# The walk of the 512-column products: runs of 16 columns from four places, or runs of 4 from thirty-two

## The chip, the cores and the metric

One core of one Trainium2 chip runs the whole program; the other cores do nothing. The metric is the device time of one execution in microseconds (us), the median of several runs. The engines of the core that matter here are TensorE (the matrix engine; its profile rows are PE for the product itself and PEld for loading the stationary operand), VectorE (DVE), ScalarE (ACT) and GpSimd (POOL). TensorE keeps one operand of 128x128 standing still, streams the columns of the other past it, and adds the result up in PSUM, whose banks hold 512 single-precision columns per partition.

## The reference

Three blocks of a transformer-like network run one after the other on one sequence of 512 positions of width 1024. Each part of a block is changed by a shift, a scale and a gate, which come from a product of a conditioning vector with a large matrix.

- A first block: a gated feed-forward part, `swiglu(y) = (silu(y @ w_gate) * (y @ w_up)) @ w_down` with a hidden width of 2816, then a mixer of four mLSTM heads and four HGRN2 heads, then a second such feed-forward part.
- A second block: gated linear attention with four heads, then `square(relu(h @ w1)) @ w2` with a hidden width of 4096.
- A third block: differential attention with eight heads and rotary positions, then the same kind of feed-forward part, then a last normalisation.

Everything is single precision. Nearly all of the arithmetic lies in products of a 512-row activation with a weight matrix; the recurrences and attention scores use many small products.

## The kernel before, in words

A large product is made in three. Each operand is split into two parts of the type float32r, a high part and a low part (the rest), and the kernel adds high by high, high by low and low by high into one PSUM bank. For weights `parts2` does the split: ScalarE copies the high part into a tile named `w` (line 118 is the helper that all ScalarE work goes through) and VectorE subtracts (line 328). Activations are kept as pairs of tiles, in the regions that the profile calls XAr and XBr.

Two functions issue these products:

- `fm` (lines 372 to 374) has a 128-column block of the weight standing and lets the 512 positions stream. Its result lies with features on partitions.
- `tm` (lines 390 to 392) has 128 positions of the activation standing and lets 512 columns of the weight stream. Its result lies with positions on partitions.

Both loop over the 128-row pieces of the contraction, three products each. Every product has its own load of a stationary operand, which runs beside the product before it. The order on TensorE is the program's order; there is no planner at run time. Background work (the conditioning products on VectorE) is put between the products by counting them, so that the order of instructions does not depend on how long a product takes.

Where the streaming operand has 512 columns, the function `runs` turns both it and the PSUM result into a view with the columns in another order. The view `(a b c) -> b a c` with a=4 and c=16 makes b=8: sixteen neighbouring columns (64 bytes) are taken from the first place, then sixteen from a place 128 columns (512 bytes) further, and so on over four places; then the four places each move on by sixteen columns. That makes 32 runs of 16. Operand and result use the same view, so that every column of the result is where it would be without it. Views of any other width are left as they are: at the beginning of most stages the positions come in two halves of 256 (`HALVES`), and the last 512 columns of the output come as two times 256; these walk straight through.

The small products (scores, transposes, recurrences) do not go through `runs`.

Of the kernel before, what the change touches and what calls it, by code (L numbers as in the profile page):

```python
# [35 lines left out]
def kernel(ctx: ExitStack, tc: tile.TileContext, a: dict, out: bass.AP):  # L36
# [321 lines left out]

    def runs(ap):

        return ap.rearrange("p (a b c) -> p b a c", a=4, c=16) if ap.shape[1] == 512 else ap

    def fm(p, wt, X, span, c=0):

        s, n = span
        kn = wt.shape[2]
        work(0.65 * kn * n / 512)
        for k in range(kn):
            xh, xl = X[k]
            wh, wl = wt[:, 0, k, c:c + 128], wt[:, 1, k, c:c + 128]  # L370
            xh, xl = runs(xh[:, s:s + n]), runs(xl[:, s:s + n])
            PE.matmul(runs(p), lhsT=wh, rhs=xh, start=k == 0, stop=False)  # L372
            PE.matmul(runs(p), lhsT=wh, rhs=xl, start=False, stop=False)  # L373
            done = PE.matmul(runs(p), lhsT=wl, rhs=xh, start=False, stop=k == kn - 1)  # L374
        products.append(done)
        if len(products) == due[0]:
            flush((1, 1, 1, 1))
# [1290 lines left out]
```

## Time and profile before

| what | value |
|---|---|
| median of 3 runs | 2318.18 us (2316.72 to 2320.07) |
| the profiled execution | 2320.75 us |
| its span, first to last instruction | 2319.0 us |
| instructions | 27,962 |
| mean granted clock of TensorE | 0.996 |
| TensorE products | busy 2262.5 us, 10,904 instructions |
| stationary loads | busy 1846.2 us, 10,904 instructions |
| VectorE | busy 1413.5 us |
| ScalarE | busy 924.0 us |
| read from HBM | 290.78 MB, 126 GB/s over the span |

The busy time of TensorE counts a product from its first fetch to a modelled end, and neighbours overlap: one product reads as 0.39 us while the next one starts 0.23 us after it. For a stream of products the useful number is therefore the distance from one start to the next. A timeline gives it: the first and the last start of a stretch, divided by the number of steps between.

### The profile page before, as it was taken

The numbers are of one execution on the slowest core, as the hardware profiler recorded it, in microseconds if no ns is written. First come the engines' busy times: TensorE is split into PE (matmuls) and PEld (weight loads), VectorE is DVE, ScalarE is ACT, GpSimd is POOL, SyncE is SP. The second block draws the span as 40 slices with busy tenths as digits, with TensorE's granted clock in tenths as the row PEclk, the third lists the DMA queues.
The fourth block names the chain that finished last, engine by engine and source line by source line (L and its number), as shares of the span: only waits on it lengthen the run. The fifth ranks groups of instructions, "written<-read, shape, count | busy, mean of one in ns | idle before, by whom it ended". The sixth has DMA issues, their size and how long they took to land.

```text
span 2319.0 us, 27962 instructions
## 1 busy us (share of the span) xinstructions
PE 2262.5 (98%) x10904; PEld 1846.2 (80%) x10904; DVE 1413.5 (61%) x2371; ACT 924.0 (40%) x1722; POOL 191.2 (8%) x126
## 2 busy tenths in 40 slices
PE   6999999999899999999999999999999999999998
PEld 4888887888788888888878887888776767888887
DVE  7846455765767746555555765658746577634364
ACT  4332224644665232234543532322435456333222
POOL 0111111000101111010000010101000100100000
PEclk9999999999999999999999999999999999999999
DMA  9755444435323655442332254445341322423231
GB/s 273 235 176 180 146 164 73 110 103 104 95 75 108 209 166 171 128 162 82 124 114 91 93 186 148 149 134 157 126 135 43 114 64 74 136 91 103 88 92 63
DMA packets 212900, 294.69 MB, mean 127 GB/s; under 512 B 7257, under 2 KB 120328, under 8 KB 212768
## 3 DMA queue, kind: packets, MB, share of 16 engines
q1 hardware_dynamic: 212128, 291.85, 41.2%
q8 instruction: 85, 1.39, 0.3%
q10 hardware_dynamic: 640, 1.07, 0.1%
q14 instruction: 47, 0.39, 0.1%
HBM read 290.78 MB, written 2.11 MB: 126 GB/s over the span
## 4 chain that ended last, share of the span: by engine, by line
PE 86%; DVE 6%; ACT 3%; DMA 2%; issue 1%; POOL 1%; POOLq 0%; SPq 0%; ACTq 0%; DVEq 0%
PE PS L392 13%; PE PS L390 13%; PE PS L391 13%; PE PS L372 13%; PE PS L373 13%; PE PS L374 13%; PE PS L1474 1%; DVE w L328 1%; POOL sm L413 1%; PE PS L907 1%; ACT RS L118 1%; PE PS L1503 1%; DMA araw<-in_ada_w_dram 1%; ACT tmp L118 1%; ACT XBf L118 1%
## 5 line engine op out<-in xcount | busy, mean ns | idle before, releaser
L328 DVE TENSOR_TENSOR w<-raw,w 128x1024 fp32r<-128x1024 f32 (+1 forms) x392 | 470.9, 1207 | 416.8 <-ACT w L118 415.8
L118 ACT ACTIVATE w<-raw 128x1024 fp32r<-128x1024 f32 (+1 forms) x392 | 389.2, 1000 | 512.3 <-PE PS L392 287.3
L373 PE MATMUL PS<-XAr,w 128*128 128x512 f32 (+1 forms) x1328 | 488.8, 368 | 0.9 <-DVE XAr L696 0.4
L374 PE MATMUL PS<-XAr,w 128*128 128x512 f32 (+1 forms) x1328 | 488.1, 368 | 0.0
L372 PE MATMUL PS<-XAr,w 128*128 128x512 f32 (+1 forms) x1328 | 485.5, 369 | 0.5 <-DVE XAr L471 0.5
L390 PE MATMUL PS<-w,XAr 128*128 128x512 f32 x806 | 319.9, 398 | 3.3 <-DVE XAr L471 2.5
L391 PE MATMUL PS<-w,XAr 128*128 128x512 f32 x806 | 318.0, 395 | 0.0
L392 PE MATMUL PS<-w,XAr 128*128 128x512 f32 x806 | 316.2, 393 | 0.0
L373 PEld LDWEIGHTS PS<-XAr,w 128*128 128x128 f32 x1328 | 251.5, 189 | 43.4 <-DVE XAr L696 1.2
L372 PEld LDWEIGHTS PS<-XAr,w 128*128 128x128 f32 x1328 | 250.4, 189 | 43.9 <-ACT XAr L118 1.3
L374 PEld LDWEIGHTS PS<-XAr,w 128*128 128x128 f32 x1328 | 251.4, 189 | 41.4
L392 PE MATMUL PS<-w,XBr 128*128 128x512 f32 x704 | 277.9, 395 | 3.0 <-DVE XBr L612 2.5
L391 PE MATMUL PS<-w,XBr 128*128 128x512 f32 x704 | 278.4, 395 | 0.0
L390 PE MATMUL PS<-w,XBr 128*128 128x512 f32 x704 | 277.7, 395 | 0.1
L118 ACT ACTIVATE tmp<-PS 128x512 f32<-128x512 f32 (+3 forms) x227 | 104.5, 466 | 416.6 <-PE PS L374 324.3
L245 DVE SCALAR_TENSOR_TENSOR acc<-araw,silu_c,acc 128x512 f32<-128x512 f32 x266 | 199.2, 749 | 70.7 <-DMA araw<-in_ada_w_dram 66.5
L253 POOL PARTITION_ALL_REDUCE tmp<-acc x38 | 133.6, 3516 | 1054.4 <-DVE acc L245 542.6
L390 PEld LDWEIGHTS PS<-w,XAr 128*128 128x128 f32 x806 | 151.9, 189 | 37.5 <-DVE XAr L471 2.7
L392 PEld LDWEIGHTS PS<-w,XAr 128*128 128x128 f32 x806 | 151.9, 189 | 34.4 <-issue 0.8
L391 PEld LDWEIGHTS PS<-w,XAr 128*128 128x128 f32 x806 | 152.1, 189 | 33.6 <-issue 1.6
L392 PEld LDWEIGHTS PS<-w,XBr 128*128 128x128 f32 x704 | 132.2, 188 | 34.1 <-DVE XBr L612 3.4
L390 PEld LDWEIGHTS PS<-w,XBr 128*128 128x128 f32 x704 | 132.1, 188 | 32.5 <-ACT RS L118 0.5
(293 smaller groups left out, 2491.1 us busy)
## 6 DMA issues: line engine op xcount, KB each, us to landing
araw<-in_ada_w_dram SPq DMA_DIRECT2D x152, 512.0 KB
raw<-in_mlp_w_dram SPq DMA_DIRECT2D x56, 1024.0 KB
raw<-in_ffn_w_gate_dram SPq DMA_DIRECT2D x20, 1024.0 KB
raw<-in_ffn_w_up_dram SPq DMA_DIRECT2D x20, 1024.0 KB
raw<-in_ffn_w_down_dram SPq DMA_DIRECT2D x20, 1024.0 KB
raw<-in_w_in_dram SPq DMA_DIRECT2D x16, 1024.0 KB
raw<-in_gla_w_in_dram SPq DMA_DIRECT2D x12, 1024.0 KB
raw<-in_diff_w_in_dram SPq DMA_DIRECT2D x12, 1024.0 KB
```

The costliest lines, as they stand in the source:

```text
L118: ins = S.activation(out, in_, func, **kw)
L245: V.scalar_tensor_tensor(acc, raw[:, k, :], col, acc, op0=ALU.mult, op1=ALU.add)
L253: G.partition_all_reduce(red, acc, channels=128, reduce_op=bass_isa.ReduceOp.add)
L328: V.tensor_tensor(wt[:, 1, ks], src[:, ks], wt[:, 0, ks].bitcast(F32), op=ALU.subtract)
L372: PE.matmul(runs(p), lhsT=wh, rhs=xh, start=k == 0, stop=False)
L373: PE.matmul(runs(p), lhsT=wh, rhs=xl, start=False, stop=False)
L374: done = PE.matmul(runs(p), lhsT=wl, rhs=xh, start=False, stop=k == kn - 1)
L390: PE.matmul(runs(p), lhsT=xh[:, s:s + 128], rhs=wh, start=n == 0, stop=False)
L391: PE.matmul(runs(p), lhsT=xh[:, s:s + 128], rhs=wl, start=False, stop=False)
L392: done = PE.matmul(runs(p), lhsT=xl[:, s:s + 128], rhs=wh, start=False, stop=n == last)
L413: G.tensor_tensor(r, ms, mhalf[:, 0:w], op=ALU.pow)
L907: PE.matmul(p[:, c * 128:(c + 1) * 128], lhsT=L[:, c * 128:(c + 1) * 128], rhs=R[:, c * 128:(c + 1) * 128], start=True, stop=True)
```

## The change

One line in `runs`. The view keeps its form, but the sizes given are b=4 and c=4, which makes a=32: four neighbouring columns (16 bytes) are taken from the first place, then four from a place 16 columns (64 bytes) further, over thirty-two places; then all places move on by four columns. That makes 128 runs of 4. Both operand and result are walked this way. Nothing else differs: the same products, the same operands, the same tiles and order.

```diff
     def runs(ap):
 
-        return ap.rearrange("p (a b c) -> p b a c", a=4, c=16) if ap.shape[1] == 512 else ap
+        return ap.rearrange("p (a b c) -> p b a c", b=4, c=4) if ap.shape[1] == 512 else ap
```

## Rows read from the trace of the kernel before

**Rows 1.** The page, part 1: busy us, share of the span, instructions.
```profile
PE 2262.5 (98%) x10904; PEld 1846.2 (80%) x10904; DVE 1413.5 (61%) x2371; ACT 924.0 (40%) x1722; POOL 191.2 (8%) x126
```
**Rows 2.** The page, part 4: the chain that ended last, by engine and by line.
```profile
PE 86%; DVE 6%; ACT 3%; DMA 2%; issue 1%; POOL 1%; POOLq 0%; SPq 0%; ACTq 0%; DVEq 0%
PE PS L392 13%; PE PS L390 13%; PE PS L391 13%; PE PS L372 13%; PE PS L373 13%; PE PS L374 13%; PE PS L1474 1%; DVE w L328 1%; POOL sm L413 1%; PE PS L907 1%; ACT RS L118 1%; PE PS L1503 1%; DMA araw<-in_ada_w_dram 1%; ACT tmp L118 1%; ACT XBf L118 1%
```
**Rows 3.** Groups by line and form, TensorE products: count, busy us, mean ns, idle.
```profile
L372 PE MATMUL PS<-XAr,w 128*128 128x512 f32 x1008 | 395.6, 396 | 0.0
L390 PE MATMUL PS<-w,XAr 128*128 128x512 f32 x794 | 316.5, 399 | 3.3 <-DVE XAr L471 2.5 <-DVE XAr L833 0.7
L390 PE MATMUL PS<-w,XBr 128*128 128x512 f32 x704 | 277.7, 395 | 0.1
L372 PE MATMUL PS<-XAr,w 128*128 128x256 f32 x320 | 89.9, 283 | 0.5 <-DVE XAr L471 0.5
L372 PE MATMUL PS<-XBr,w 128*128 128x512 f32 x208 | 81.7, 393 | 0.0
```
**Rows 4.** PE waits, longest in total first: us, times, longest.
```profile
PE PS L907 <- DVE tmp L935: 8.2, 3, 7.0
PE PS L209 <- DMA tmp<-in_ffn_pre_g_dram: 6.2, 1, 6.2
```
**Rows 5.** Timeline, `fm` streaming XA: first and last of 176 rows (start, us).
```profile
299.67 0.39 PE L374 MATMUL PS<-XAr,w 128*128 128x512 f32 x1
...
339.93 0.39 PE L372 MATMUL PS<-XAr,w 128*128 128x512 f32 x1
```
**Rows 6.** Timeline, `tm` with XB standing: first and last of 156 rows.
```profile
229.81 0.40 PE L390 MATMUL PS<-w,XBr 128*128 128x512 f32 x1
...
265.81 0.40 PE L392 MATMUL PS<-w,XBr 128*128 128x512 f32 x1
```
**Rows 7.** Timeline, `tm` with XA standing: first and last of 153 rows.
```profile
2074.72 0.39 PE L392 MATMUL PS<-w,XAr 128*128 128x512 f32 x1
...
2109.80 0.39 PE L391 MATMUL PS<-w,XAr 128*128 128x512 f32 x1
```
**Rows 8.** Timeline, seven products in a row near 1700 us.
```profile
1698.09 0.63 PE L391 MATMUL PS<-w,XAr 128*128 128x512 f32 x1
...
1700.65 0.63 PE L391 MATMUL PS<-w,XAr 128*128 128x512 f32 x1
```
**Rows 9.** Windows: PE, PEld, DVE, ACT, POOL busy (x), granted clock, DMA share, GB/s.
```profile
1697.80:1701.10 3.30, 3.30 (x10) 2.53 (x9) 3.01 (x7) 1.02 (x2) 0.00 (x0) 0.50 0.55 159
225.00:268.00 43.00, 43.00 (x187) 34.74 (x186) 24.72 (x30) 7.95 (x8) 7.29 (x2) 1.00 0.52 168
270.00:356.00 86.00, 86.00 (x375) 70.49 (x374) 47.29 (x62) 26.08 (x34) 16.45 (x25) 1.00 0.48 159
```
**Rows 10.** Timeline, `fm` in halves of 256, straight: first and last of 156 rows.
```profile
1334.78 0.28 PE L372 MATMUL PS<-XAr,w 128*128 128x256 f32 x1
...
1352.96 0.28 PE L374 MATMUL PS<-XAr,w 128*128 128x256 f32 x1
```
**Rows 11.** Timeline, `tm` on 256 columns, straight: first and last of 36 rows.
```profile
2307.66 0.28 PE L390 MATMUL PS<-w,XAr 128*128 128x256 f32 x1
...
2311.86 0.27 PE L392 MATMUL PS<-w,XAr 128*128 128x256 f32 x1
```
**Rows 12.** Timeline, `fm` in gated linear attention: first and last of 89 rows.
```profile
1184.54 0.39 PE L374 MATMUL PS<-XAr,w 128*128 128x512 f32 x1
...
1205.07 0.39 PE L372 MATMUL PS<-XAr,w 128*128 128x512 f32 x1
```

## The prediction

> **What bounds the kernel now.** I read the page from the top. TensorE is busy for 98% of the span, VectorE for 61%, ScalarE for 40% [rows 1], so the first question is whether TensorE waits for anybody. The chain that ended last lies on TensorE for 86%, and six lines of `fm` and `tm` hold 13% each, 78% together [rows 2]. The list of waits agrees: the largest are 8.2 and 6.2 us [rows 4]. So the time is the number of products times the distance from one start to the next, and the page's mean of 0.39 us is not that distance, since neighbours overlap.
>
> The number comes from the groups by form. `fm` has 1008 + 208 products of 512 columns on line 372, `tm` has 794 + 704 on line 390 [rows 3]; each stands on three lines, so 3648 and 4494, together 8142. The distance comes from the timeline. Streaming XA, `fm` makes 175 steps in 339.93 - 299.67 = 40.26 us, 0.2301 us each [rows 5]. `tm` makes 155 steps in 36.00 us with XB standing, 0.2323 [rows 6], and 152 in 35.08 us with XA standing, 0.2308 [rows 7]; weighted with the counts 0.2315. 8142 products at about 0.231 us are 1880 us, 81% of the span. A step of 1 ns in that distance is worth 8.1 us.
>
> Then the question that decides: does a product take longer than its columns? Where the granted clock is 0.50 (1.2 GHz), six steps take 1700.65 - 1698.09 = 2.56 us, 0.4267 each [rows 8, 9]: 512 columns at one per cycle, to the last nanosecond. At 2.4 GHz the same would be 0.2133. The stretches at a granted 1.00 [rows 9] show 0.2301 and 0.2315, so 16.8 and 18.2 ns of a product are lost at the high level that are not lost at the low one. The 32 runs of the walk are there at both levels, so the loss is a supply that falls short of one column per cycle at 2.4 GHz. On that supply the order of the columns can act.
>
> **The change part by part.** No instruction is removed, added or moved: the same products and loads, the same bytes into the same places of PSUM, so that DMA, VectorE and ScalarE have the same work. The only term is the distance of 8142 products.
>
> No row shows runs of 4, so I bound them. From below: the whole loss goes, 3648 x 16.8 ns + 4494 x 18.2 ns = 61 + 82 = 143 us. From above: the whole loss is the price of the 32 runs, 0.53 and 0.57 ns each; 96 more runs then cost 50.4 and 54.6 ns, 184 + 245 = 429 us.
>
> Between these ends the nearest rows are the products that walk straight. `fm` on 256 columns makes 155 steps in 18.18 us, 0.1173 each [rows 10]; `tm` on 256 makes 35 in 4.20 us, 0.1200 [rows 11]. If what is lost grows with the columns, 512 straight columns would take 0.2346 and 0.2400, more than the 0.2301 and 0.2315 of the walk. Runs would then help: from one run of 512 down to 16 is five halvings of the run's length, which brought 4.5 and 8.5 ns, 0.9 and 1.7 a halving. From 16 to 4 is two more, 1.8 and 3.4 ns: 3648 x 1.8 + 4494 x 3.4 = 6.6 + 15.3 = 21.9 us. I take this value. The reason is rows 8: a stream that is complete at half the rate has no fixed cost per product or run that shows, and a loss that only appears at the full rate should grow with the columns. It is a reading by analogy and I hold it weakly.
>
> Of product time 78 of 81 parts lie in the chain, so I count 0.97 of it, 21.3 us. Nothing that hides it is late next: in the saturated stretches VectorE is busy 24.72 of 43 us and 47.29 of 86, DMA 0.52 and 0.48 [rows 9], so a stream shorter by 1% meets no new wait. The profiled execution took 2320.75 us (span 2319.0 and 1.75 around it); less 21.3 it is 2299.5. The median of the runs is 2.6 us below the profiled one, so on its scale 2296.9, and I forecast 2297.
>
> [...]
>
> **The rivals.**
> *The walk doesn't matter.* The loss could come from the loads of the next stationary operand, which run beside each product and are not changed. For it: the same walk takes 0.2308 or 0.2323 depending on which region stands [rows 6, 7]. Against it: a load is there at 1.2 GHz too, and nothing is lost. Time 2318, within 4.6 us.
>
> *The two streams settle in a worse rhythm.* With the same form, tile names and walk, one stretch takes 88 steps in 20.53 us, 0.2333 each [rows 12], and not the 0.2301 of rows 5. So the distance is not fixed by the walk alone; product and load seem to lock into one phase or another. If the new walk puts all products at 0.2333, `fm` loses 3.2 ns and `tm` 1.8: 11.7 + 8.1 = 19.8 us, 2338. The place is every saturated stream; it decides from the point where 0.2301 and 0.2315 are passed.
>
> *Each run has a price.* If the loss of straight products is fixed for each product and doesn't grow with columns, 512 straight ones would take 0.1173 + 0.1067 = 0.2240 in `fm` and 0.1200 + 0.1067 = 0.2267 in `tm`, and 32 runs cost 6.1 and 4.8 ns, 0.19 and 0.15 a run. 96 more: 18.2 and 14.4 ns, 66 + 65 = 131 us, 2449. For it: the jump to a new place is the one thing the change multiplies by four. Against it: at half the rate 32 runs cost nothing. It decides as soon as a run costs anything, and at a third of that price it is already at 2362.
>
> **How the numbers follow.** My forecast, a gain by shorter runs, has 0.43, with its own range from 2268 (twice the step) to 2313. No difference has 0.21; about 0.2%, 4.6 us, is what a measurement of this kernel can tell from none. The worse rhythm has 0.20, between 2323 and 2365. The price per run has 0.16; it spreads from 2340 to 2747, and a quarter of it lies under 2400. The range is 2268 to 2400: it leaves out 0.05 below, for a stream nearer to its lower bound, and 0.12 above. Faster is 0.43, same 0.21, slower 0.36.
>
> **What would show it.** The start-to-start distance in the stretches of rows 5 to 7 is the whole test: 0.228 in both kinds says the forecast, 0.2301 and 0.2315 unchanged says the first rival, 0.233 in both the second, 0.245 or more the third. The products of 256 columns must stay at 0.1173 and 0.1200, at least where nothing else changes, and the waits of TensorE must stay a few us each, as must the granted clock. A loss that is large in `fm` and small in `tm`, or the other way round, would say that the side counts on which the weights stand. The prediction is wrong if the distances rise, and wrong in its reason if the time falls while they don't.

## The result, and the profile after

The changed kernel takes 2287.72 us (median of 4 runs, 2284.43 to 2289.16) where the one before took 2318.87 in the same comparison: a ratio of 0.9865, 95% interval 0.9848 to 0.9882, or 31 us less. That is inside the range of the prediction and on its side; the step was 31 us where 21 were forecast. The profiled executions lie 34.4 us apart in their spans, 2319.0 and 2284.6 us, and the rows below are theirs.

The page of the changed kernel, parts 1 and 4 (answers to [rows 1, 2]):

```profile
span 2284.6 us, 27962 instructions
...
PE 2225.5 (97%) x10904; PEld 1839.5 (81%) x10904; DVE 1416.6 (62%) x2371; ACT 923.5 (40%) x1722; POOL 190.2 (8%) x126
...
PE 85%; DVE 6%; ACT 3%; DMA 2%; issue 2%; POOL 1%; POOLq 0%; SPq 0%; ACTq 0%; DVEq 0%
```

The number of instructions is the same, and so are the busy times of VectorE, ScalarE and GpSimd to about 3 us. The order of TensorE's products is the same too. What is gone is 37 us of TensorE's busy time in products. TensorE's idle time, the span less its busy time, rose from 2319.0 - 2262.5 = 56.5 us to 2284.6 - 2225.5 = 59.1.

The distances from start to start, in timelines of the changed kernel (start us, us, then the row). First `fm` streaming XA, first and last of 178 rows, which answers to [rows 5]:

```profile
274.77 0.39 PE L374 MATMUL PS<-XAr,w 128*128 128x512 f32 x1
...
314.80 0.39 PE L374 MATMUL PS<-XAr,w 128*128 128x512 f32 x1
```

177 steps in 40.03 us: 0.2262 each, where it was 0.2301. Then `tm` with XB standing, first and last of 177 rows, which answers to [rows 6]: 176 steps in 40.07 us, 0.2277 where it was 0.2323.

```profile
221.79 0.39 PE L390 MATMUL PS<-w,XBr 128*128 128x512 f32 x1
...
261.86 0.39 PE L392 MATMUL PS<-w,XBr 128*128 128x512 f32 x1
```

`tm` with XA standing answers to [rows 7], and here one number is not enough. First and last of 161 rows, of 92 rows, and of 104 rows:

```profile
2044.64 0.38 PE L391 MATMUL PS<-w,XAr 128*128 128x512 f32 x1
...
2079.84 0.38 PE L392 MATMUL PS<-w,XAr 128*128 128x512 f32 x1
...
2251.71 0.39 PE L390 MATMUL PS<-w,XAr 128*128 128x512 f32 x1
...
2272.80 0.39 PE L391 MATMUL PS<-w,XAr 128*128 128x512 f32 x1
...
446.63 0.39 PE L392 MATMUL PS<-w,XAr 128*128 128x512 f32 x1
...
469.81 0.39 PE L390 MATMUL PS<-w,XAr 128*128 128x512 f32 x1
```

The three stretches make 160 steps of 0.2200, 91 of 0.2318 and 103 of 0.2251: the same lines, the same tile names, the same walk, and three rhythms, each kept through the rows shown. Of the 15 stretches of over 40 such products one goes from 0.2251 to 0.2318 near its end; the others keep one of the three but for their first products. Before, all of them ran at 0.2307 to 0.2314.

The straight products of 256 columns did not move. Here 119 rows of them, the first one and the 512-column product that follows the last:

```profile
1321.83 0.28 PE L373 MATMUL PS<-XAr,w 128*128 128x256 f32 x1
...
1335.79 0.38 PE L372 MATMUL PS<-XAr,w 128*128 128x512 f32 x1
```

13.96 us over 119 is 0.1173, as in [rows 10].

The sum closes. The mean distance, taken over all pairs of 512-column products less than 0.3 us apart, went in `fm` from 230.24 to 226.38 ns streaming XA (3 x 1008 products) and from 230.63 to 226.67 streaming XB (3 x 208), in `tm` from 231.14 to 225.19 with XA standing (3 x 794) and from 232.18 to 227.93 with XB standing (3 x 704): 11.7 + 2.5 + 14.2 + 9.0 = 37.4 us. Less the 2.6 us of added idle time that is 34.8; the spans differ by 34.4.

### The profile page after: what moved, and what is told of

Same layout as the page of the kernel before. It is cut to its first block, busy times and chain, and to the rows that moved or that the text cites. A ratio compares the mean times of both kernels' runs of the same rounds, so it can differ in the third digit from the quotient of the medians.

```text
span 2284.6 us, 27962 instructions
## 1 busy us (share of the span) xinstructions
PE 2225.5 (97%) x10904; PEld 1839.5 (81%) x10904; DVE 1416.6 (62%) x2371; ACT 923.5 (40%) x1722; POOL 190.2 (8%) x126
## 4 chain that ended last, share of the span: by engine, by line
PE 85%; DVE 6%; ACT 3%; DMA 2%; issue 2%; POOL 1%; POOLq 0%; SPq 0%; ACTq 0%; DVEq 0%
PE PS L392 13%; PE PS L390 13%; PE PS L391 13%; PE PS L372 13%; PE PS L373 13%; PE PS L374 13%; PE PS L1474 1%; DVE w L328 1%; ACT RS L118 1%; DMA araw<-in_ada_w_dram 1%; POOL sm L413 1%; PE PS L907 1%; PE PS L1503 1%; ACT tmp L118 1%; ACT w L118 1%
## 5 line engine op out<-in xcount | busy, mean ns | idle before, releaser
L373 PE MATMUL PS<-XAr,w 128*128 128x512 f32 (+1 forms) x1328 | 482.2, 363 | 1.0 <-DVE XAr L472 0.6
L374 PE MATMUL PS<-XAr,w 128*128 128x512 f32 (+1 forms) x1328 | 481.2, 363 | 0.0
L372 PE MATMUL PS<-XAr,w 128*128 128x512 f32 (+1 forms) x1328 | 480.2, 365 | 0.1
L390 PE MATMUL PS<-w,XAr 128*128 128x512 f32 x806 | 314.3, 391 | 3.2 <-DVE XAr L471 2.2
L391 PE MATMUL PS<-w,XAr 128*128 128x512 f32 x806 | 312.2, 387 | 0.0
L392 PE MATMUL PS<-w,XAr 128*128 128x512 f32 x806 | 310.6, 386 | 0.0
L392 PE MATMUL PS<-w,XBr 128*128 128x512 f32 x704 | 274.3, 390 | 4.1 <-DVE XBr L612 3.6
L391 PE MATMUL PS<-w,XBr 128*128 128x512 f32 x704 | 274.2, 389 | 0.0
L390 PE MATMUL PS<-w,XBr 128*128 128x512 f32 x704 | 274.0, 390 | 0.1
```

The lines of the kernel that those rows point to most:

```text
L390: PE.matmul(runs(p), lhsT=xh[:, s:s + 128], rhs=wh, start=n == 0, stop=False)
L391: PE.matmul(runs(p), lhsT=xh[:, s:s + 128], rhs=wl, start=False, stop=False)
L392: done = PE.matmul(runs(p), lhsT=xl[:, s:s + 128], rhs=wh, start=False, stop=n == last)
```

## The experiments

Each kernel is the changed one with one thing altered, its time set against the kernel before on the same chip. They order TensorE's products as it does, but for the two with small loads and the one with walked halves. For each I give the distance of a long stretch of `fm` streaming XA, which the reader can compare with 0.2301 before and 0.2262 after, and the loss, which is that distance less 0.2133 (an estimate: half of the 0.4267 us that 512 columns took at a granted clock of 0.50 [rows 8, 9]).

### Straight products

```diff
-        return ap.rearrange("p (a b c) -> p b a c", b=4, c=4) if ap.shape[1] == 512 else ap
+        return ap
```

> The views are left out: all products of 512 columns walk straight, operand and result. Theory A (mine: a loss that grows with the columns and shrinks with shorter runs): 0.2346 us a product in fm and 0.2400 in tm, total near 2373 us. Theory B (the loss of straight products is fixed for each product, and each run costs something; the gain of the change would then need another reason): 0.2240 and 0.2267, total near 2275. Theory C (product and load of the next stationary operand lock into a rhythm, and the walk only shifts which): several values side by side in one kernel, between 0.220 and 0.240, total anywhere from 2275 to 2375.

Measured: 2339.31 us, ratio 1.009 [1.0075, 1.0106]. `fm`, first and last of 172 rows:

```profile
299.75 0.39 PE L373 MATMUL PS<-XAr,w 128*128 128x512 f32 x1
...
339.81 0.39 PE L373 MATMUL PS<-XAr,w 128*128 128x512 f32 x1
```

171 steps in 40.06 us, 0.2343. Theory A said 0.2346, so in `fm` the loss does grow with the columns: twice the 0.1173 of a straight 256. Theory B, with its 0.2240, falls. In `tm` theory A said 0.2400 and the timelines give 0.2333 with XA standing (172 steps in 40.13 us) and 0.2340 with XB (163 in 38.14). The 36 products of [rows 11] are no measure for `tm` as a whole. So the walk of 16 was worth 20 us over straight, the walk of 4 another 31.

### Operand alone, result alone

```diff
     def runs(ap):
         return ap.rearrange("p (a b c) -> p b a c", b=4, c=4) if ap.shape[1] == 512 else ap
+    def runs_r(ap):
+        return ap
...
-            PE.matmul(runs(p), lhsT=wh, rhs=xh, start=k == 0, stop=False)
+            PE.matmul(runs_r(p), lhsT=wh, rhs=xh, start=k == 0, stop=False)
```

(the same for all six products; the second kernel has the two functions' bodies exchanged)

> The streaming operand is walked in runs of 4 from thirty-two places, the result straight, so that the columns of each product's result stand in another order. If the read side of the stream is what the walk helps: as the changed kernel, 0.2262 in fm, 0.2245 to 0.228 in tm, total 2288 within 6 us. If the write side in PSUM is: as the kernel whose products walk straight.

> The result is walked in runs of 4 from thirty-two places, the streaming operand straight, so that the columns of each product's result stand in another order. If the read side counts: as the kernel whose products walk straight (theory A 2373). If the write side counts: 2288 within 6 us. If writes off the straight order cost something, it shows here as a time above the straight kernel's.

These two serve for their time alone: the columns that are read and written no longer match, so what they compute is something else.

Measured: operand alone 2287.14 us, 0.9865 [0.9848, 0.9882]; result alone 2335.56, 1.0073 [1.0058, 1.0089]. First and last of 179 rows with the operand walked:

```profile
299.67 0.39 PE L376 MATMUL PS<-XAr,w 128*128 128x512 f32 x1
...
339.92 0.39 PE L377 MATMUL PS<-XAr,w 128*128 128x512 f32 x1
```

First and last of 172 rows with the result walked:

```profile
299.80 0.39 PE L377 MATMUL PS<-XAr,w 128*128 128x512 f32 x1
...
339.86 0.39 PE L377 MATMUL PS<-XAr,w 128*128 128x512 f32 x1
```

178 steps of 0.2261 and 171 of 0.2343: the changed kernel's distance and the straight one's. The whole effect lies in the order in which the streaming operand is read from SBUF. The order of writing in PSUM, in runs of 4 from places 64 bytes apart, neither helps nor costs in the distance: 0.2343 walked and straight. (The kernel with the result walked is 4 us faster than the straight one. Its distances are the same to 0.1 ns in all four forms, so that difference is not the stream's.)

### Runs of 4, and the distance between the places

```diff
-        return ap.rearrange("p (a b c) -> p b a c", b=4, c=4) if ap.shape[1] == 512 else ap
+        return ap.rearrange("p (a b c) -> p b a c", a=4, c=4) if ap.shape[1] == 512 else ap
```

(512 bytes apart; b=2, c=4 gives 32 bytes, b=8 128 and b=16 256)

> Runs of 4 as in the changed kernel, but from four places 512 bytes apart as in the kernel before; operand and result alike. If only the length of a run counts (theory A): 0.226 in fm and 0.2245 to 0.228 in tm, 2288 within 6 us. If the distance of 64 bytes between places counts: back towards 0.2301 and 0.2315, 2318.

> Runs of 4 from sixty-four places 32 bytes apart, operand and result alike. The loss of a product over its 0.2133 us was 20.9 ns straight, 12.9 ns with places 64 bytes apart and 53.4 ns with places 512 bytes apart (fm, XA). If it is the distance between neighbouring reads that counts and a longer one is worse: between straight and 64 bytes, 0.226 to 0.234, total 2288 to 2340. If what counts is that neighbouring reads fall on different parts of the memory, with 512 bytes falling on the same part: 0.226 or less, total 2288 or less.

> Runs of 4 from sixteen places 128 bytes apart, operand and result alike. If the loss grows with the distance between neighbouring reads: between the 0.2262 us of 64 bytes and the 0.267 of 512, about 0.235, total near 2360. If only some distances fall on the same part of the memory: 0.226 as with 64 bytes, total 2288 within 15 us.

> Runs of 4 from eight places 256 bytes apart, operand and result alike. If the loss grows with the distance beyond 64 bytes: between the 0.2465 us of 128 bytes and the 0.267 of 512, near 0.257, total near 2510. If 64 bytes are one good distance among bad ones without an order: anything from 0.226 to 0.267.

First and last rows of `fm` streaming XA with the places 32 bytes apart (175 rows):

```profile
299.61 0.40 PE L372 MATMUL PS<-XAr,w 128*128 128x512 f32 x1
...
339.92 0.39 PE L372 MATMUL PS<-XAr,w 128*128 128x512 f32 x1
```

128 bytes apart (164 rows):

```profile
319.71 0.41 PE L373 MATMUL PS<-XAr,w 128*128 128x512 f32 x1
...
359.92 0.41 PE L374 MATMUL PS<-XAr,w 128*128 128x512 f32 x1
```

256 bytes apart (146 rows):

```profile
349.59 0.44 PE L374 MATMUL PS<-XAr,w 128*128 128x512 f32 x1
...
389.98 0.45 PE L372 MATMUL PS<-XAr,w 128*128 128x512 f32 x1
```

512 bytes apart (152 rows):

```profile
319.63 0.43 PE L372 MATMUL PS<-XAr,w 128*128 128x512 f32 x1
...
359.89 0.43 PE L373 MATMUL PS<-XAr,w 128*128 128x512 f32 x1
```

| step from one 16 bytes to the next | distance, us | loss, ns | time, us | ratio to before |
|---|---|---|---|---|
| 16 bytes (straight) | 0.2343 | 21.0 | 2339.31 | 1.009 [1.0075, 1.0106] |
| 32 | 40.31/174 = 0.2317 | 18.4 | 2328.27 | 1.0046 [1.0031, 1.0061] |
| 64 (the change) | 0.2262 | 12.9 | 2287.72 | 0.9865 [0.9848, 0.9882] |
| 128 | 40.21/163 = 0.2467 | 33.4 | 2433.87 | 1.0501 [1.0484, 1.0519] |
| 256 | 40.39/145 = 0.2786 | 65.3 | 2674.83 (one run) | none |
| 512 | 40.26/151 = 0.2666 | 53.3 | 2587.99 | 1.1162 [1.1145, 1.1179] |

This refutes what theory A says of the run's length. Five kernels have runs of 4; their losses go from 12.9 to 65.3 ns, so among them something else counts. It goes with the step between places, and 64 bytes are a valley: 31 us under the walk of before, while 128 bytes would have cost 116. Beyond 64 the loss does not grow with the step, since 256 is worse than 512. In `tm` with XA standing 64 bytes are best too: the mean distances, in the order of the table, are 0.2333, 0.2332, 0.2252, 0.2501, 0.2784 and 0.2680.

Two limits of the table are to be kept in mind. The product has 2048 bytes in each partition, so a longer step means fewer places and more jumps back to the first place: 4 in 128 runs at 64 bytes, 16 at 256, 32 at 512. No kernel changes one without the other, and 512 may come out under 256 for that reason. And operand and result were walked together; that the loss at the other steps lies with the operand, as the gain at 64 bytes does, was not tried.

Even the 512-byte step adds nothing at the low clock. A timeline of that kernel, and a window with its granted clock (PE, PEld, DVE, ACT, POOL, clock, DMA share, GB/s):

```profile
31.98 0.63 PE L373 MATMUL PS<-XAr,w 128*128 128x512 f32 x1
32.40 0.63 PE L374 MATMUL PS<-XAr,w 128*128 128x512 f32 x1
32.83 0.63 PE L373 MATMUL PS<-XAr,w 128*128 128x512 f32 x1
33.26 0.54 PE L374 MATMUL PS<-XAr,w 128*128 128x512 f32 x1
```

```profile
30.20:33.40 3.20, 3.20 (x8) 2.53 (x9) 2.17 (x5) 0.00 (x0) 0.00 (x0) 0.50 1.17 291
```

Three steps in 1.28 us are 0.427 each at 0.50, no more than the 0.4267 of the walk of 16 at that clock. With places 256 bytes apart four steps from 32.28 to 33.99 us are 0.4275 each; in the same place of the program the kernel before makes four from 32.09 to 33.80, at a granted 0.50, and they are 0.4275 too. So in these three walks, runs of 16 and runs of 4 with steps of 256 and 512 bytes, the differences between 0.2301, 0.2786 and 0.2666 show at a granted 1.00 alone.

### Loads of the next stationary operand

```diff
+            if k == 0:
+                PE.matmul(runs(p), lhsT=wh, rhs=xh, start=True, stop=False)
+            PE.matmul(runs(p[0:32]), lhsT=wh[:, 0:32], rhs=xl, start=False, stop=False)
+            PE.matmul(runs(p[0:32]), lhsT=wl[:, 0:32], rhs=xh, start=False, stop=False)
+            if k > 0:
+                done = PE.matmul(runs(p), lhsT=wh, rhs=xh, start=False, stop=k == kn - 1)
```

(in place of the three products of `fm`; `tm` in the same way; the second kernel with `runs` returning `ap`)

> The changed kernel's walk; two of the three products of each step load only 32 of the 128 columns of their stationary operand and fill 32 partitions of the result, so that half of the load columns are left and most of the low-part terms are left out. Theory D (the stream loses where the load of the next stationary operand reads beside it): the loss over 0.2133 us falls to about a half, near 0.220 us a product, total near 2240. Theory E (the stream loses by its own order of reads): 0.226 us stays, total 2288 within 6 us.

> The same small loads, with the products walking straight. Theory D: the loss of 20.9 ns falls to about 10, 0.2238 us a product, total near 2256, and the walk is worth only half of what it is worth with whole loads. Theory E: 0.234 us stays, total 2339 within 6 us.

Measured: 2274.53 us, 0.9813 [0.9798, 0.9827], and straight 2322.77, 1.0021 [1.0012, 1.003]. First and last rows of `fm` streaming XA, walked (180 rows) and then straight (173):

```profile
274.66 0.38 PE L374 MATMUL PS<-XAr,w 128*32 128x512 f32 x1
...
314.94 0.38 PE L377 MATMUL PS<-XAr,w 128*128 128x512 f32 x1
```

```profile
274.79 0.40 PE L377 MATMUL PS<-XAr,w 128*128 128x512 f32 x1
...
314.78 0.40 PE L373 MATMUL PS<-XAr,w 128*128 128x512 f32 x1
```

With half of the load columns gone, these are 179 steps in 40.28 us, 0.2250, and 172 in 39.99, 0.2325. So the loss falls from 12.9 to 11.7 ns and from 21.0 to 19.2: about a tenth where theory D asked for a half. Neither theory has it alone, but E is nearer: most of the loss is the stream's own, and the loads add to it. How much they add is less sure than the half makes it look. A load of 32 columns is recorded as 108 ns and one of 128 as 188, so the time of the loads fell by 28% only; if the loss goes with that time, a third of it would be theirs, by this estimate. The small products also fill fewer partitions of the result, which was not tried apart. Between the two the walk is worth 48 us, as with whole loads (52).

With XA standing, `tm` no longer shows its rhythms of 0.2200 and 0.2318: the means of its 16 stretches of over 40 products lie between 0.2237 and 0.2248. That makes it likely that the rhythms come from the loads meeting the stream; no run takes it further.

### Runs of 8, runs of 2

```diff
-        return ap.rearrange("p (a b c) -> p b a c", b=4, c=4) if ap.shape[1] == 512 else ap
+        return ap.rearrange("p (a b c) -> p b a c", b=2, c=8) if ap.shape[1] == 512 else ap
```

(and b=8, c=2)

> Runs of 8 from thirty-two places 64 bytes apart, operand and result alike: of two steps from one 16 bytes to the next, one is 16 bytes long and one 48. If the loss is a sum over single steps (16 bytes 0.163 ns, 32 bytes 0.146, 64 bytes 0.101, from the kernels straight, 32 and 64 bytes apart): 128 x 0.14 = 18 ns, 0.2314 us a product, total near 2322. If the length of the run is what counts where the places are 64 bytes apart: one halving from 16 and one above 4, near 0.228, total near 2303.

> Runs of 2 from thirty-two places 64 bytes apart, operand and result alike: the distance of the changed kernel, half its run. If shorter runs help by themselves (the halvings of the forecast): 0.2245 us a product or less, total near 2275. If every step of 64 bytes costs the 0.101 ns that it costs with runs of 4, 256 steps lose 26 ns: 0.239, total near 2393. If a visit of 8 bytes can't be read ahead in time: clearly above 0.25, total over 2480.

Measured: runs of 8 2322.53 us, 1.0025 [1.0015, 1.0034]. First and last of 175 rows of `fm` streaming XA:

```profile
299.75 0.39 PE L373 MATMUL PS<-XAr,w 128*128 128x512 f32 x1
...
339.77 0.39 PE L373 MATMUL PS<-XAr,w 128*128 128x512 f32 x1
```

174 steps in 40.02 us, 0.2300, and 0.2334 with XA standing in `tm`. The time that the sum over single steps gave was 2322, but its distance was 0.2314: `fm` lies under it and `tm` over it, and the total agrees because the two cancel. I don't take it for a law also because the walk of before has 3 steps of 16 bytes for each jump and would lose 96 x 0.163 + 32 x 0.417 = 29 ns by the same sum (0.417 from 53.3 ns over 128 steps); it lost 16.8.

Runs of 2: 3935.45 us, 1.7005 [1.697, 1.704]. First and last of 93 rows:

```profile
499.70 0.61 PE L372 MATMUL PS<-XAr,w 128*128 128x512 f32 x1
...
539.87 0.62 PE L374 MATMUL PS<-XAr,w 128*128 128x512 f32 x1
```

92 steps in 40.17 us, 0.4366 a product (mean granted clock of the execution 0.998), 1.71 ns for each of its 256 visits of 8 bytes. The same kernel at the low clock, first and last of 6 rows and their window:

```profile
1026.58 0.61 PE L373 MATMUL PS<-XAr,w 128*128 128x512 f32 x1
...
1028.76 0.61 PE L372 MATMUL PS<-XAr,w 128*128 128x512 f32 x1
```

```profile
1026.60:1029.00 2.40, 2.40 (x7) 1.76 (x6) 1.87 (x3) 2.11 (x5) 0.00 (x0) 0.50 0.24 93
```

Five steps in 2.18 us are 0.436 at 0.50, the same as at 1.00: with runs of 2 the doubled clock brings nothing, and even the low level loses 9 ns against 0.4267. What limits this stream does not follow TensorE's clock. A run of 4 took 0.2262 / 128 = 1.77 ns for its 16 bytes in the changed kernel, and would have 1.67 at 0.2133. So by this estimate a visit takes about 1.7 ns whether two or four columns are fetched by it, and a stream in runs of 4 would then have just that and nothing to spare. Operand and result were walked together here; that it is the operand, as with runs of 4, was not tried.

### Halves walked as well

```diff
-        return ap.rearrange("p (a b c) -> p b a c", b=4, c=4) if ap.shape[1] == 512 else ap
+        return ap.rearrange("p (a b c) -> p b a c", b=4, c=4) if ap.shape[1] in (256, 512) else ap
```

> The changed kernel, with the products of 256 columns walked as well, in runs of 4 from sixteen places 64 bytes apart. There are 1284 of them at 0.1173 to 0.1200 us. If the gain is one of the stream's own order of reads, they go to half of the 0.2262 of the 512-column ones, near 0.1135: 5 to 6 us less, total near 2282. If a stretch of halves is too short or waits for other engines: 2288.

Measured: 2301.18 us, 0.9938 [0.9925, 0.9951], 13 us more than the changed kernel. (Its profiled execution took 2307.71 us, the longest of the five.) First and last of 39 rows of halves:

```profile
397.57 0.27 PE L372 MATMUL PS<-XAr,w 128*128 128x256 f32 x1
...
401.92 0.28 PE L374 MATMUL PS<-XAr,w 128*128 128x256 f32 x1
```

The products did most of what was expected of them: 38 steps in 4.35 us, 0.1145, where 0.1135 was expected and 0.1173 is the straight distance. The time is lost around them. A window in the first such stage, this kernel first and then the changed one:

```profile
403.00:410.50 7.50, 1.26 (x7) 0.85 (x7) 6.26 (x12) 5.66 (x12) 1.17 (x2) 0.82 0.88 167
```

```profile
403.00:410.50 7.50, 6.36 (x54) 6.16 (x52) 5.58 (x10) 4.72 (x12) 1.83 (x3) 1.00 0.78 132
```

TensorE works 1.26 of 7.5 us instead of 6.36, and its granted clock falls, to a mean of 0.82. What it waits for is in the list of waits of this stage, again this kernel and then the changed one:

```profile
PE PS L459 <- DVE Y L445: 6.2, 1, 6.2
```

```profile
PE PS L459 <- DVE Y L445: 1.5, 1, 1.5
```

The instructions of this kernel stand in another order: transposes of the next activations (line 459) come before halves that the changed kernel still has ahead of them, and they wait for VectorE. Over the span this wait grows from 5.7 to 14.1 us, and the granted clock has a mean of 0.85, 0.87 and 0.92 in three windows over stages of halves where the changed kernel has 1.00. Why the order came out another is not shown. So the run doesn't tell what walked halves are worth in the same order; that was not tried.

## Why the prediction was right, and what in it was not

**What bounds the kernel.** Right. Distance times count explains what the span lost to within a microsecond, nothing new is waited for (the largest waits are 8.1 and 6.2 us, where they were 8.2 and 6.2), and the other engines' busy times stayed.

**The loss as a supply that falls short at the full clock.** Right as far as the runs go: with the operand alone in another order the whole gain is there (0.2261 us against 0.2343 straight), and at a granted 0.50 the worst steps tried, 256 and 512 bytes, take no longer than the walk of before (0.4275 and 0.427 against 0.4275 and 0.4267). Only runs of 2 take longer there as well (0.436). No run shows a clock in GHz: what the prediction calls 1.2 and 2.4 GHz are the granted 0.50 and 1.00, and its 0.2133 us is an estimate, half of the 0.4267 measured at 0.50.

**The loss grows with the columns.** Right for `fm` (0.2346 forecast, 0.2343 measured), too much for `tm` (0.2400 against 0.2333 and 0.2340). The term rested on 35 steps at the end of the kernel.

**"From 16 to 4 is two more" halvings.** This step was wrong in kind, although its sign came out. It gave `fm` 1.8 ns and `tm` 3.4; the trace gives 3.9, and 4.3 to 5.9. The runs of 4 at other steps lose more than the runs of 16 did (18.4 to 65.3 ns against 16.8), so a rule on the length of the run alone can't be the reason. What counts is which address follows which, and 64 bytes is the best step of those tried. That the forecast had the right sign is luck: with the same reasoning it would have been wrong by more than a hundred microseconds had the change been b=8 in place of b=4. (A slip without weight: 0.97 of 21.9 us is 21.2, not 21.3.)

**The rivals.** That the walk doesn't matter is refuted: with the walk alone altered, the kernels take from 2287 to 3935 us. The rhythms are real: three of them stand side by side in `tm`. They are not fixed by the walk and the order of the products: with the operand alone walked, where both are the same, the last long stretch of `tm` makes 100 steps in 22.00 us, 0.2200, and in the changed kernel 96 in 22.24, 0.2317. The price of this rival, every product at 0.2333, was not paid, since two of the three rhythms are below before's; and the stretch of [rows 12], which it rested on, went from 0.2333 to 0.2263 (89 steps in 20.14 us). A price for each run rested on a straight product of 0.2240, and 0.2343 was measured. A jump does have a price where the step is bad: 128 runs, most of them 256 bytes from the last, lose 65.3 ns, 0.51 each, about the 0.53 that I set as the upper end. It is not paid at 64 bytes, where 128 runs lose less than 32 did (12.9 ns against 16.8).

**The bounds.** The lower one, the whole loss gone, was approached only by the 0.2200 rhythm of `tm`; 6.7 ns are left there of the 17.5 that this form lost before.

What stays open: why 64 bytes is the valley and 256 the peak, and what the jumps back add to either, why the 16-byte run with rare long jumps loses less than its steps taken singly, and what decides which rhythm a stretch falls into.

## What to carry to other kernels

Where products of this type follow one another without a gap, look at the distance from start to start and set it against the columns at the granted clock; what was over here was a supply that fell short, and the order of reading the streaming operand was a lever on it that cost no instruction (0.2343 us straight, 0.2301 and 0.2262 in the two walks). Keep whole runs of 16 bytes (runs of 2 cost 72% more time in all than runs of 4), try the step between them on the chip rather than reason on it, and let the result's order follow whatever the operand needs: in runs of 4 from places 64 bytes apart, the one case tried apart, it cost nothing (0.2343 us walked and straight). When a part is made faster, look whether the order of the instructions stayed: the halves went from 0.1173 to 0.1145 us, the order changed, and the kernel became 13 us slower.

## What the runs showed of the hardware that I had not expected

- The loss of a stream goes with the step from one 16 bytes to the next, and not in order of it: per product over 0.2133 us 21.0 ns at 16 bytes, 18.4 at 32, 12.9 at 64, 33.4 at 128, 65.3 at 256, 53.3 at 512 (operand and result walked together; at 64 bytes the operand alone does it).
- Runs of 2 single-precision columns from places 64 bytes apart took 0.4366 us a product where runs of 4 took 0.2262, and the clock did not matter to them: 0.4366 at 1.00 and 0.436 at 0.50.
- The result's order in PSUM, in runs of 4 from places 64 bytes apart, is free: 0.2343 walked and straight.
- Streams of products keep to a rhythm for nearly all of a stretch: in `tm` with XA standing 0.2200, 0.2251 or 0.2318 us with the same code.
